# Turning cached keys on VectorE instead of TensorE, and an earlier split of the samples' sums, in a hybrid streaming layer

## The chip, the cores and the metric

The kernel runs on one core of one Trainium2 chip. A core has five engines that work in parallel, each through its own instructions in order: TensorE (PE in the profile; its weight loads are PEld), VectorE (DVE), ScalarE (ACT), GpSimd (POOL) and SyncE (SP), which here issues nearly all DMA transfers. The metric is the device time of one execution in microseconds (us), the median of several runs.

## The reference

One step of one encoder layer for two streams at once: 512 prompt frames without a cache, and 64 sample frames with 512 cached frames. Cut to the parts around the change:

```python
def stick_breaking(q, k, v, q_pos, k_pos):
    z = einsum('bqhd,bkhd->bhqk', q, k) / sqrt(HEAD_DIM)          # float32
    mask = k_pos[None, :] < q_pos[:, None]
    log_1mb = where(mask, log_sigmoid(-z), 0.0)
    after = cumsum(log_1mb, axis=3, reverse=True) - log_1mb
    w = where(mask, exp(log_sigmoid(z) + after), 0.0)
    return einsum('bhqk,bkhd->bqhd', w, v)

hn = rmsnorm(x, g_norm1)
q, k, v, gb, gc, hc = split(hn @ w_in)          # 8 heads x 128; 1024 convolution channels
q, k = rmsnorm(q, g_q), rmsnorm(k, g_k)
o_attn = stick_breaking(q, concat(k_past, k), concat(v_past, v), ...)
o_conv = gb * causal_conv3(gc * hc)
x = x + concat(rmsnorm(o_attn), rmsnorm(o_conv)) @ w_out
x = x + (silu(h2 @ w_gate) * (h2 @ w_up)) @ w_down                # h2 = rmsnorm(x)
```

The model width is 2048 and the feed-forward width 5632. Everything is float32. The cached keys come as `cache_k` with 512 frames x 8 heads x 128 and are already normed.

## The kernel before

Frames lie along the free axis (576 = 512 + 64 columns, two halves of 288), channels along the 128 partitions. A float32 matrix is split into a high part of reduced precision (a cast on ACT) and a remainder (a subtraction on DVE), and a product is three matmuls of parts; the helper `split` (lines 226 to 229) does cast and subtraction. Time passes in three stages: the input projection, then attention together with the output projection, then the feed-forward network.

PE's instructions stand in the order in which the program writes them. Those of the other engines are ordered by a scheduler when the kernel is built. PE's order is made by a small queue of generators, `Pipeline`: each group of three projection matmuls (line 223) is one tick, and a generator that yields n is resumed n ticks later.

In the attention stage the convolution half of the output projection supplies the ticks: products `pjo` of `mixc` with the weights `whi` and `wlo`. One generator `attend(h)` runs per head, a new one every 29 ticks. For the prompt it makes scores in blocks of 128 keys, block 2 together with 3 first (tile `z2`), then 1 (`z1`) and 0 (`z0`), takes a softplus of each on ACT (three activations, lines 1116 to 1118) and DVE (line 1119), masks and sums on POOL, and splits the results (`ph`, `pl`). Then it makes the samples' scores `zs` (line 1189) against the new keys and the cached keys `kcT`, and their softplus and running sums in `sp` (tile `hbl`; POOL lines 1193 to 1197). Later the sums along the keys are made by matmuls with triangular matrices (lines 1223 to 1243 for the prompt, 1204 to 1207 for the samples, from the split sums `sph` and `spl`), `weights(b)` masks on DVE (line 1214), takes the Exp on ACT (line 1216) and splits again, and the values are weighed (`po`, line 1268, and line 1282).

`split_qk` splits the queries and keys of the next head into `qh`, `ql`, `kh`, `kl`. `load_cached_keys(h)` brings a head's cached keys with one DMA as four blocks of 128 frames x 128 channels into `cK`. `keys_cached(h)` (line 1140) turns these blocks to channels x frames by four transposes on PE into a PSUM tile, copies that to `kcT` on ACT (line 1143) and asks for the keys of the next head. For the first head it is called after the scores of block 1, for each later one from the head before it, between the samples' softplus and the sums. The samples' sums are split behind the weights of block 1.

SP has eight semaphores for its transfers in turn, so a transfer waits for the landing of the eighth before it, and whatever stands behind a waiting request on SP waits too.

Of the kernel before, what the change touches and what calls it, by code (L numbers as in the profile page):

```python
# [10 lines left out]
F32 = mybir.dt.float32  # L11
# [5 lines left out]
P = 128  # L17
TP = 512
TS = 64
T = TP + TS  # L20
HALF = T // 2
HALVES = ((0, HALF), (HALF, T))
D = 2048
KD = D // P
NH = 8
# [10 lines left out]
NFP = NFF // 2  # L36
DC = D // 256
SLOTS = 7
# [63 lines left out]
def tile_hybrid_stream_step(  # L102
# [6 lines left out]
    nc = tc.nc  # L109
# [3 lines left out]
    ck, cv = cache_k[0, 0], cache_v[0, 0]  # L113
# [23 lines left out]
    ps_pj = ctx.enter_context(tc.tile_pool(name="ps_pj", bufs=3, space=PSUM))  # L137
    ps_z = tc.alloc_tile_pool(name="ps_z", bufs=1, space=PSUM)

    def misc(name):  # L140
        return ps_z.tile([P, 512], F32, tag="misc", name=name, bufs=2)
# [3 lines left out]
    for half in (1, 0):  # L145
        for c in range(D // 256):
            specs.append((w_out[half * AW : (half + 1) * AW, c * 256 : (c + 1) * 256]
# [46 lines left out]
    def next_weight():  # L194
        i = pos[0]
        pos[0] += 1
        end = first_block
        def pieces_of(j):
            hi, lo = weight_split(j)
            for a in range(0, 2048, 512):  # L200
                weight_parts(raws[j][:, :2048], hi, lo, a, a + 512, nc.vector)
                yield 7

        while len(raws) < min(i + 2, end):
            load_weight()
        if len(ready) <= i:
            split_weight(nc.vector)
        while len(raws) < min(i + 3, end):
            load_weight()
        if i + 1 < end:  # L210
            pipe.spawn(pieces_of(i + 1))
            pipe.run_due()
        out = ready[i]
        ready[i] = None
        return out
# [10 lines left out]
    def split(hi, lo, src, lo_eng=None):  # L226
        cast = nc.scalar.copy(out=hi, in_=src)  # L227
        (lo_eng or nc.vector).tensor_tensor(out=lo, in0=src, in1=hi.bitcast(F32), op=ALU.subtract)  # L228
        return cast.ins
# [6 lines left out]
    ident = const.tile([P, P], F32, name="ident")  # L236
# [312 lines left out]
    def turn_x(kt, low=None):  # L549
# [25 lines left out]
        if q == 0:  # L575
            for (a, b), d in zip(HALVES, (b11[:, j], b12a[:, j] if j < NP - 1 else b12b)):
                nc.scalar.activation(out=d[:, 0, :], in_=st[:, 0, a:b], func=AF.Copy, scale=g)
# [54 lines left out]
    with tc.manual_schedule(engines={mybir.EngineType.Activation, mybir.EngineType.DVE, mybir.EngineType.SP}):  # L632
# [60 lines left out]
        for kt in range(KD + LAG):  # L693
# [22 lines left out]
            if kt in (7, 11, 17):  # L716
                j = (kt - 7) // 4
# [7 lines left out]
        for c in range(2):  # L725
            for i, (a, b) in enumerate(HALVES):
                if i:
# [12 lines left out]
        for kt in range(KD):  # L740
# [6 lines left out]
            if kt == 9:  # L747
                nc.vector.reduce_sum(out=ssr, in_=ssx, axis=mybir.AxisListType.X)
                nc.vector.tensor_scalar(out=ssr, in0=ssr, scalar1=1.0 / D, scalar2=EPS, op0=ALU.mult, op1=ALU.add)
                nc.gpsimd.tensor_tensor(out=rst, in0=ssr, in1=nhalf, op=ALU.pow)  # L750
# [15 lines left out]
    for c in range(2):  # L766
        for i, (a, b) in enumerate(HALVES):
            nc.scalar.copy(out=e1[c][:, a:b], in_=v1ps[c][i])
# [81 lines left out]
    def group_scale(acc_, bufs):  # L850
        for a, b in HALVES:
            ss = misc("ssg")[:, :HALF]
            mm(ss, oner.bitcast(F32), acc_[:, a:b], start=True, stop=True)
            yt = tmp.tile([P, 2, HALF], F32, tag="hl", name="ytg", bufs=bufs)
            y, t = yt[:, 0], yt[:, 1]
            nc.scalar.activation(out=ss, in_=ss, func=AF.Identity, scale=1.0 / (8 * P), bias=epsc)
            nc.scalar.activation(out=y, in_=ss, func=AF.Ln)
            nc.scalar.activation(out=y, in_=y, func=AF.Exp, scale=-0.5)
            nc.scalar.activation(out=t, in_=y, func=AF.Square)
            nc.vector.scalar_tensor_tensor(out=t, in0=t, scalar=-0.5, in1=ss, op0=ALU.mult, op1=ALU.mult)  # L860
            nc.vector.scalar_tensor_tensor(out=acc_[:, a:b], in0=t, scalar=1.5, in1=y, op0=ALU.add, op1=ALU.mult)
            yield 1
# [11 lines left out]
    def a_done(n, c, i, ps, part):  # L874
        kind, g = UNITS[n][:2]
        a, b = HALVES[i]
        if kind in ("v", "qk"):
# [125 lines left out]
    bpool = tc.alloc_tile_pool(name="bpool", bufs=1, reuse_waits="tile", side="left")  # L1003
    qf, kf = (bpool.tile([P, T], F32, name=name) for name in ("qf", "kf"))
    qh, ql, kh, kl = (bpool.tile([P, TP], F32R, name=name) for name in ("qh", "ql", "kh", "kl"))
    cK = bpool.tile([P, 4, P], F32, name="cK")
    ws = bpool.tile([P, 320], F32, name="ws")
    kcT = bpool.tile([P, TP], F32, name="kcT")
    neg1r, trir = (bpool.tile([P, P], F32R, name=name) for name in ("neg1r", "trir"))
# [4 lines left out]
    sph, spl = (bpool.tile([P, T], F32R, name=name) for name in ("sph", "spl"))  # L1014
# [9 lines left out]
    def split_qk():  # L1024
        split(qh, ql, qf[:, :TP])
        split(kh, kl, kf[:, :TP])

    def load_cached_keys(h):
        nc.sync.dma_start(out=cK, in_=ck[:, h, :].rearrange("(i p) d -> p i d", p=P))

    def fetch_v(h):
        nc.sync.dma_start(out=vtok, in_=v_dram[h])
# [2 lines left out]
    load_qk(0)  # L1035
    split_qk()
    load_cached_keys(0)
    fetch_v(0)
    nc.vector.tensor_scalar(out=neg1r, in0=ident, scalar1=0.0, scalar2=-1.0, op0=ALU.mult, op1=ALU.add)
# [27 lines left out]
    for h in range(NH):  # L1067
        t = tpool.tile([P, 2, T], F32R, tag=f"t{h}", name=f"mixa{h}")
# [5 lines left out]
    def out_proj(frame, R, after=None, before=None, first=None):  # L1074
        for c in range(D // 256):
            whi, wlo = first[0] if first and c == 0 else next_weight()
            load_x2()
            if before:
                before(c)
            for j in range(2):  # L1080
                kt = 2 * c + j
                for a, b in HALVES:
                    if first and kt == a == 0:
                        ps = first[1]
                    else:
                        ps = ps_pj.tile([P, HALF], F32, tag="pj", name="pjo")
                        product(ps, whi, wlo, slice(j * P, (j + 1) * P), frame, 8, a, b)
                    if first and c < PLAIN:
                        nc.vector.tensor_tensor(out=x2(kt)[:, a:b], in0=ps, in1=R[:, a:b], op=ALU.mult)
                        continue  # L1090


                    def finish_out(wait, ps=ps, kt=kt, a=a, b=b):
                        yield wait
                        nc.vector.tensor_tensor(out=ps, in0=ps, in1=R[:, a:b], op=ALU.mult)
                        nc.vector.tensor_tensor(out=x2(kt)[:, a:b], in0=ps, in1=x2(kt)[:, a:b], op=ALU.add)

                    pipe.spawn(finish_out(3 if after and kt == a == 0 else 0))
                    pipe.run_due()
                if first and j and c < PLAIN:  # L1100
                    nc.gpsimd.dma_start(out=x2t[c], in_=xt_dram[2 * c : 2 * c + 2].rearrange("k p t -> p k t"),
                                        accum_op=ALU.add)
                if after:
                    after(kt)
# [32 lines left out]
        split(bt["vh"][2], bt["vl"][2], vtok[:, 2, :])  # L1137

    def keys_cached(h):
        kc = ps_pj.tile([P, 512], F32, tag="pj", name="kc")  # L1140
        for i in range(4):
            nc.tensor.transpose(kc[:, i * P : (i + 1) * P], cK[:, i, :], ident)
        nc.scalar.copy(out=kcT, in_=kc)
        if h + 1 < NH:
            load_cached_keys(h + 1)

# [3 lines left out]
    def attend(h):  # L1150
        pr, ph, pl, s1h, s1l, sp = (bt[n] for n in ("pr", "ph", "pl", "s1h", "s1l", "sp"))
# [60 lines left out]
        def weights(b):  # L1212
            for i in ((2, 3) if b == 2 else (b,)):
                nc.vector.scalar_tensor_tensor(out=zb[i][:, :P], in0=zb[i][:, :P], scalar=0.0, in1=mneg,
                                               op0=ALU.min, op1=ALU.add)
            nc.scalar.activation(out=pr[b][:, : full[b]], in_=z[b][:, : full[b]], func=AF.Exp)
            return split(ph[b], pl[b], pr[b][:, : width[b]])

        yield 1
        if h + 1 < NH:  # L1220
            keys_cached(h + 1)
        yield 2
        mm(zb[3], trif, pb[3], stop=False, **kw)
        mm(zb[2][:, P:], neg1f, pb[3], stop=False, **kw)
        mm(zb[2], trir, ph[2], stop=False, **kw)
# [1 line left out]
        behind = weights(2)  # L1227
        if h + 1 < NH:
            with tc.issue_after(behind):
                split_qk()  # L1230
        yield 4
        mm(zb[1], trir, ph[1], stop=False, **kw)
        mm(zb[1], trir, pl[1], stop=False, **kw)
        mm(zb[1][:, P:], neg1r, s1h, stop=False, **kw)
        mm(zb[1][:, P:], neg1r, s1l, stop=True, **kw)
        behind = weights(1)
        with tc.issue_after(behind):
            split(sph, spl, sp)
        yield 4
        mm(zb[0], trir, ph[0], stop=False, **kw)  # L1240
        mm(zb[0], trir, pl[0], stop=False, **kw)
# [50 lines left out]
    def heads():  # L1292
        yield 9
        open_b()
        yield 3
        for h in range(NH):
            pipe.spawn(attend(h))
            yield PERIOD
# [86 lines left out]
    def before_b2(c):  # L1385
        if c == 3:
            load_columns([("B", 0), ("B", 1)])
        elif c == D // 256 - 2:
            load_columns([("A", 0)])
# [305 lines left out]
```

## Time and profile before

| | us |
|---|---|
| median of 3 runs | 2347.15 |
| lowest and highest | 2346.91, 2348.15 |
| the profiled execution, its own time | 2347.48 |
| its span | 2345.8 |
| PE busy in the span | 2332.0 (99%) |
| DVE busy | 1940.0 (83%) |
| ACT busy | 1239.2 (53%) |
| POOL busy | 294.2 (13%) |

The span runs from the first to the last instruction of the profiled execution. Busy times of engines overlap. The granted clock of TensorE was 1.0 as a mean of the execution. The heads' matmuls lie between about 585 and 760 us.

A row of a timeline has the start from the beginning of the span, the length, the engine, the source line, the operation, the tile written and those read, the shapes, and in brackets the idle time of the engine before it and what ended it. Matmuls are pipelined: one lasts longer than the distance to the next one's start.

### The profile page before, as it was taken

Reading aid. Unit: us, or ns where it says so; the run is one execution under the profiler, and the core shown is the slowest. Engines: PE = TensorE matmul, PEld = TensorE weight load, DVE = VectorE, ACT = ScalarE, POOL = GpSimd, SP = SyncE. Lnnn points to the kernel's source line nnn. Section 1 sums busy time; section 2 is a strip of 40 time slices with the busy share of each in tenths; the row PEclk is TensorE's granted clock in tenths of the full one; section 3 lists DMA queues with packets and bytes.
Section 4 is the critical chain, followed back from the end, with each engine's and each line's share of the span. In section 5 each row is a group of like instructions: output and inputs, shape, how many; then the busy total and the mean of one; then the engine's idle time right before and its main releaser. Section 6 shows DMA issues by size and latency. Waiting matters only on the chain. (4 is left out here: it accounts for less than half of the span.)

```text
span 2345.8 us, 43802 instructions
## 1 busy us (share of the span) xinstructions
PE 2332.0 (99%) x17561; PEld 2321.6 (99%) x17561; DVE 1940.0 (83%) x2834; ACT 1239.2 (53%) x2244; POOL 294.2 (13%) x374
## 2 busy tenths in 40 slices
PE   9999999999999999999999999999999999999999
PEld 8999999999999999999999999999999999999998
DVE  8889889797777898888888888888888778887875
ACT  8556656455887564444444444444444444444454
POOL 0211121120332320000000000000000002431211
PEclk9999999999999999999999999999999999999999
DMA  8444243436753454444444444444444937875642
GB/s 270 137 122 123 90 142 103 149 116 208 202 143 109 168 198 126 154 141 136 154 128 149 148 134 149 138 139 153 127 150 140 356 112 229 231 218 187 201 130 82
DMA packets 482867, 368.85 MB, mean 157 GB/s; under 512 B 11630, under 2 KB 465064, under 8 KB 482664
## 3 DMA queue, kind: packets, MB, share of 16 engines
q1 hardware_dynamic: 475848, 356.58, 47.5%
q0 software_dynamic: 6384, 9.21, 2.3%
q8 instruction: 137, 2.24, 0.4%
q14 instruction: 66, 0.54, 0.1%
q10 hardware_dynamic: 432, 0.27, 0.0%
HBM read 285.52 MB, written 80.49 MB: 156 GB/s over the span
## 5 line engine op out<-in xcount | busy, mean ns | idle before, releaser
L228 DVE TENSOR_TENSOR whl<-raw_a,whl 128x1024 fp32r<-128x1024 f32 (+4 forms) x384 | 435.8, 1135 | 61.2 <-ACT whl L227 59.9
L404 PE MATMUL psy<-t,whl 128*128 128x288 f32 x3000 | 449.8, 295 | 0.0
L227 ACT CAST whl<-raw_a 128x1024 fp32r<-128x1024 f32 (+4 forms) x384 | 360.0, 939 | 137.7 <-PE psx L404 46.4
L404 PE MATMUL psy<-h_s,whl 128*128 128x288 f32 x2766 | 417.4, 295 | 0.6 <-ACT part L427 0.6
L404 PEld LDWEIGHTS psy<-t,whl 128*128 128x128 f32 x3000 | 414.8, 188 | 0.2
L404 PE MATMUL psw<-t,whl 128*128 128x288 f32 x2688 | 390.3, 295 | 0.0
L404 PEld LDWEIGHTS psy<-h_s,whl 128*128 128x128 f32 x2766 | 383.7, 188 | 1.2 <-ACT part L427 1.1
L404 PEld LDWEIGHTS psw<-t,whl 128*128 128x128 f32 x2688 | 367.0, 188 | 0.2
L228 DVE TENSOR_TENSOR whl<-raw_b,whl 128x1024 fp32r<-128x1024 f32 (+5 forms) x234 | 253.3, 1083 | 88.0 <-ACT whl L227 87.1
L227 ACT CAST whl<-raw_b 128x1024 fp32r<-128x1024 f32 (+5 forms) x234 | 211.0, 904 | 211.0 <-issue 75.2
L427 ACT COPY part<-psy 128x288 f32<-128x288 f32 x309 | 122.8, 397 | 345.0 <-PE psy L404 343.8
L404 PE MATMUL psx<-h_s,whl 128*128 128x288 f32 x1164 | 170.9, 295 | 0.0
L227 ACT CAST whl<-s 128x1024 fp32r<-128x1024 f32 (+5 forms) x103 | 95.2, 925 | 122.8 <-PE psw L404 115.0
L404 PEld LDWEIGHTS psx<-h_s,whl 128*128 128x128 f32 x1164 | 159.8, 188 | 0.0
L404 PE MATMUL psy<-t12a,whl 128*128 128x288 f32 x1056 | 150.9, 296 | 0.0
L404 PE MATMUL psw<-t34a,whl 128*128 128x288 f32 x1056 | 150.6, 295 | 0.0
L404 PEld LDWEIGHTS psy<-t12a,whl 128*128 128x128 f32 x1056 | 143.5, 188 | 0.3
L404 PEld LDWEIGHTS psw<-t34a,whl 128*128 128x128 f32 x1056 | 143.7, 188 | 0.0
L228 DVE TENSOR_TENSOR whl<-s,whl 128x1024 fp32r<-128x1024 f32 (+5 forms) x103 | 109.8, 1066 | 20.2 <-ACT whl L227 19.5
L1439 POOL DMA_DIRECT2D hid_dram<-form x7 | 5.2, 738 | 954.1 <-DVE form L228 945.8
L223 PE MATMUL pjo<-mixc,whi 128*128 128x288 f32 x512 | 119.0, 300 | 0.0
L223 PE MATMUL pjo<-mixa,whi 128*128 128x288 f32 x512 | 102.8, 296 | 0.0
(591 smaller groups left out, 3953.3 us busy)
## 6 DMA issues: line engine op xcount, KB each, us to landing
hid_dram<-form SPq DMA_DIRECT2D x147, 288.0 KB, 2.8
raw_a<-in_w_in_dram SPq DMA_DIRECT2D x22, 1024.0 KB, 5.5
raw_b<-in_w_in_dram SPq DMA_DIRECT2D x22, 1024.0 KB, 6.1
raw_b<-in_w_gate_dram SPq DMA_DIRECT2D x22, 1024.0 KB, 7.8
raw_b<-in_w_up_dram SPq DMA_DIRECT2D x22, 1024.0 KB, 6.5
raw_a<-in_w_gate_dram SPq DMA_DIRECT2D x22, 1024.0 KB, 5.8
raw_a<-in_w_up_dram SPq DMA_DIRECT2D x22, 1024.0 KB, 5.5
h_s<-hid_dram SPq DMA_DIRECT2D x10, 2016.0 KB, 11.0
```

The lines of the kernel that those rows point to most:

```text
L223: mm(ps, w_[:, k, csl], x_[:, a:b], start=(k == 0 and n == 0), stop=(k == nk - 1 and n == 2))
L227: cast = nc.scalar.copy(out=hi, in_=src)
L228: (lo_eng or nc.vector).tensor_tensor(out=lo, in0=src, in1=hi.bitcast(F32), op=ALU.subtract)
L404: mm(ps, whl[:, w_, j, :], x_, start=(start and j == 0 and q == 0), stop=(j == len(xs_) - 1 and q == 2), skip_group_check=True)
L427: nc.scalar.copy(out=t, in_=st["y"])
L1439: q.dma_start(out=hid_dram[fp][2 * n - 2 : 2 * n].rearrange("f p t -> p f t"), in_=t.bitcast(F32))
```

## The change

Three things change.

1. The cached keys of a head are loaded by four DMAs instead of one. DMA number g/32 brings channels g to g+31 of all 512 frames, in pieces of 32 numbers (128 bytes), so that `cK` holds 4 x 16 blocks of 32 frames x 32 channels, each where its turned form belongs.
2. One DVE instruction, `nc.vector.transpose`, turns all blocks of 32 x 32 in place and writes `kcT`. The four transposes on PE, the PSUM tile `kc` and the copy on ACT are gone.
3. In `attend`, `keys_cached(h + 1)` is called after the weights of block 2 and after the split of the samples' sums, and that split stands behind the Exp and cast of block 2 instead of block 1. The two yields of 1 and 2 ticks become one of 3; ticks do not move.

```diff
+BK = 32
-    cK = bpool.tile([P, 4, P], F32, name="cK")
+    cK = bpool.tile([P, TP], F32, name="cK")
     def load_cached_keys(h):
-        nc.sync.dma_start(out=cK, in_=ck[:, h, :].rearrange("(i p) d -> p i d", p=P))
+        for g in range(0, P, BK):
+            nc.sync.dma_start(out=cK[g : g + BK].rearrange("j (t d) -> j t d", d=BK),
+                              in_=ck[:, h, g : g + BK].rearrange("(t j) d -> j t d", j=BK))
     def keys_cached(h):
-        kc = ps_pj.tile([P, 512], F32, tag="pj", name="kc")
-        for i in range(4):
-            nc.tensor.transpose(kc[:, i * P : (i + 1) * P], cK[:, i, :], ident)
-        nc.scalar.copy(out=kcT, in_=kc)
+        nc.vector.transpose(out=kcT, in_=cK)
         if h + 1 < NH:
             load_cached_keys(h + 1)
...
-        yield 1
-        if h + 1 < NH:
-            keys_cached(h + 1)
-        yield 2
+        yield 3
         mm(zb[3], trif, pb[3], stop=False, **kw)
...
         if h + 1 < NH:
             with tc.issue_after(behind):
                 split_qk()
+        with tc.issue_after(behind):
+            split(sph, spl, sp)
+        if h + 1 < NH:
+            keys_cached(h + 1)
         yield 4
         mm(zb[1], trir, ph[1], stop=False, **kw)
...
-        behind = weights(1)
-        with tc.issue_after(behind):
-            split(sph, spl, sp)
+        weights(1)
         yield 4
```

`tc.issue_after(behind)` keeps what is recorded inside it behind the instruction `behind`, here the cast of the block's Exp.

## The prediction

> **What bounds the kernel now.** I read the page first, then the busy time of the attention stretch, then TensorE's (PE's) waits there, then the timelines of single engines.
>
> ```profile
> span 2345.8 us, 43802 instructions
> PE 2332.0 (99%) x17561; PEld 2321.6 (99%) x17561; DVE 1940.0 (83%) x2834; ACT 1239.2 (53%) x2244; POOL 294.2 (13%) x374
> ```
>
> PE is busy for all but 13.8 us of the span. The profiled execution took 2347.48 us, 1.7 us more than its span and 0.33 us more than the median of the runs (2347.15 us). I make the sum against the profiled execution and carry its difference over to the median. The edit touches only the 180 us in which the eight heads run between the output projection's matmuls:
>
> ```profile
> 580.00:760.00 180.00, 178.13 (x1301) 172.57 (x1300) 133.69 (x280) 141.22 (x319) 57.22 (x106) 1.00 0.53 157
> ```
>
> The columns are the stretch, its length and the busy time of PE, weight loads, DVE, ACT and POOL, then granted clock, DMA share, GB/s. PE leaves 1.9 us idle; DVE is busy 74% of the time, ACT 78%. So time can be won here only by giving PE fewer instructions or by ending its waits. The waits (total, times, longest):
>
> ```profile
> PE zs L1205 <- DVE spl L228: 1.0, 3, 0.4
> PE z L1161 <- DVE kl L228: 0.3, 1, 0.3
> PE zs L1204 <- ACT sph L227: 0.3, 1, 0.3
> ```
>
> **Part 1, the 32 transposes on PE go.** One head's set in PE's timeline (start, length):
>
> ```profile
> 617.65 0.30 PE L223 MATMUL pjo<-mixc,whi 128*128 128x288 f32 x1
> 617.78 0.60 PE L1142 MATMUL kc<-ident,cK 128*128 128x128 f32 x4
> 618.13 0.38 PE L223 MATMUL pjo<-mixc,whi 128*128 128x288 f32 x1
> 618.35 0.30 PE L223 MATMUL pjo<-mixc,wlo 128*128 128x288 f32 x1
> ```
>
> Projection matmuls follow each other by 0.13 us (617.65 to 617.78). With the set between them, the next but one starts 0.57 us after 617.78; without it, 0.13 us after. A set costs 0.44 us, eight cost 3.5 us. PE's written order is otherwise untouched. The copy out of PSUM goes from ACT too:
>
> ```profile
> L1143 ACT COPY kcT<-kc x8: 561/576/583, 591.9 to 724.2; 128x512 f32<-128x512 f32 x8
> ```
>
> That frees 0.58 us of ACT a head, which is not the bound, and I count it at nothing.
>
> **Part 2, the samples' split moves ahead of the second block.** `spl` is what PE waits for at L1205 and `sph` at L1204. In heads 1 to 6 the changed build has `sph` directly behind `kh` on ACT and `spl` directly behind `kl` on DVE, so both leave their queues before the Exp, cast and subtraction of block 1, about 1 us earlier. The waits were at most 0.4 us each: 1.3 us gone. What is late next there is `kl`:
>
> ```profile
> 625.21 0.68 DVE L228 TENSOR_TENSOR kl<-kf,kh 128x512 fp32r<-128x512 f32 x1
> 626.17 0.28 PE L1161 MATMUL z<-qh,kl 128*128 128x256 f32 x1
> ```
>
> It ends at 625.89, 0.28 us before PE uses it, and nothing new stands ahead of it in those heads. The gain side is therefore 3.5 + 1.3 = 4.8 us, 0.20% of the time, and it cannot be much more, since all of PE's idle time in the stretch is 1.9 us.
>
> **Part 3, the transposes on DVE.** No DVE transpose is in this trace. The nearest rows are DVE instructions on as many float32 elements, such as the 0.68 us above. I take 0.69 us. Below I allow 0.5 us, since a copy reads one operand and not two; above, 2.4 us, in case the turn takes four such passes, which no row excludes. From the third on, the transpose also waits until PE has read the old `kcT`, with `s0l` and block 0's maximum queued behind it on DVE; the built order puts it just ahead of `s0l`.
>
> ```profile
> 613.23 1.06 PE L1189 MATMUL zs<-qf,kcT 128*128 128x64 f32 x8
> 616.36 0.56 DVE L228 TENSOR_TENSOR s0l<-hbl,s0h 128x384 fp32r<-128x384 f32 x1 [1.39 <-ACT s0h L227]
> ```
>
> PE is done reading at 614.3, and DVE sits idle for 1.39 us until 616.36: that gap covers 0.69 us, and the wait with it. Without that cover the transpose would push `s0l` and what follows by its own length. In head 0 there are two on the path.
>
> The first: scores of the samples need `kcT`, and DVE reaches the transpose behind the split of block 2.
>
> ```profile
> 591.75 0.42 DVE L228 TENSOR_TENSOR hbe<-pr,hbe 128x256 fp32r<-128x256 f32 x1 [1.11 <-ACT hbe L227]
> 592.85 1.06 PE L1189 MATMUL zs<-qf,kcT 128*128 128x64 f32 x8
> ```
>
> It runs from 592.17 to 592.86. PE, 0.44 us earlier than before, wants the result at 592.41: a wait of 0.45 us, which eats the first set's gain.
>
> The second is behind the split of block 1, and here the order of head 0 matters. Casts of q and k for head 1, which stood ahead of the Exps of blocks 1 and 0, are now placed by the scheduler behind them. In the changed build, ACT's order from the samples' cast on is
>
> ```
> sph, Exp z1, ph1, qh, Exp z0, kh
> ```
>
> and DVE's is
>
> ```
> spl, pl1, transpose, z0 mask, evacuation, wlo, ql, kl
> ```
>
> PE's scores of head 1 need `kh` and `kl`, so they now hang on a chain that begins with POOL's sums for the samples, which stood behind them before:
>
> ```profile
> 601.56 1.70 POOL L1197 TENSOR_TENSOR hbl<-hbl 128x64 f32<-128x64 f32 x3
> 603.05 0.62 ACT L227 CAST kh<-kf 128x512 fp32r<-128x512 f32 x1
> 603.57 0.48 ACT L1216 ACTIVATE hbl<-z 128x384 f32<-128x384 f32 x1
> 604.08 0.51 ACT L227 CAST ph<-hbl 128x384 fp32r<-128x384 f32 x1
> 604.50 0.67 ACT L227 CAST sph<-hbl 128x576 fp32r<-128x576 f32 x1
> 604.40 0.68 DVE L176 TENSOR_TENSOR wlo<-raw_a,whi 128x512 fp32r<-128x512 f32 x1
> 605.00 0.55 DVE L228 TENSOR_TENSOR pl<-hbl,ph 128x384 fp32r<-128x384 f32 x1
> 606.14 0.28 DVE L1214 SCALAR_TENSOR_TENSOR z<-z,mneg 128x128 f32<-128x128 f32 x1
> 606.34 0.44 DVE L1089 TENSOR_TENSOR x<-pjo,accc 128x288 f32<-128x288 f32 x1
> 605.66 0.28 PE L1161 MATMUL z<-qh,kh 128*128 128x256 f32 x1
> 605.78 0.27 PE L1161 MATMUL z<-qh,kl 128*128 128x256 f32 x1
> ```
>
> POOL is done at 603.3. From there, by the distances between starts in these rows: `sph` to 603.9, Exp z1 to 604.4, `ph1` to 604.9 on ACT; `pl1` from 605.0 to 605.5 and the transpose to 606.1 on DVE; the z0 mask to 606.3, evacuation to 606.7, `wlo` to 607.3, `ql` to 607.9, `kl` to 608.6. (On ACT, Exp z0 and `kh` end at 607.6, so PE's first score would start then and stop again for `kl`.) PE wants `kl` at 605.78 less 0.44, at 605.34. The stall is 608.6 less 605.34, 3.3 us. Were all of ACT and DVE a little earlier in head 0 it would be 2; if POOL's sums slip, which hang on a softplus that now stands behind a weight cast, 4.5. I take 3.3.
>
> **Part 4, the loads.** One request of 512 pieces of 512 bytes becomes four requests with 2048 pieces of 128 bytes in all.
>
> ```profile
> cK<-in_cache_k_dram SPq DMA_DIRECT2D x8, 256.0 KB, 2.9
> raw_a<-in_w_in_dram SPq DMA_DIRECT2D x22, 1024.0 KB, 5.5
> SPq L1029 <- PE kc L1142: 15.8, 6, 3.2
> 581.77 0.43 SPq L1029 DMA_DIRECT2D cK<-in_cache_k_dram  x1
> ```
>
> The weight load in the second row is 2048 pieces of 512 bytes (128 columns of float32). So four times as many pieces land in 2.9 to 5.5 us, and three more issues of SP at 0.43 us come on top: 4.2 to 6.8 us. A head's keys are asked for when the head before has been turned, some 20 us earlier, so I count it at nothing; in head 0 the second load has the 12 us from 592.9 to 605.5. On SP, the requests behind the keys' (q, k and weights of the next head) now wait for DVE instead of PE, at nearly the same moments. The Trainium skill, "DMA: Bandwidth & Descriptors", section "Specifications", speaks against the smaller pieces: full rate wants at least 512 bytes. By that rule a load would be dearer; with the cover of 12 us the sum would stay as it is even at twice 5.5 us.
>
> **Sum.** -3.5 - 1.3 + 0.45 + 3.3 = -1.05 us. From the median of 2347.15 us that makes **2346.1 us**, 0.04% faster. About 0.2% (4.7 us) is what a measurement of this kernel can tell from no change.
>
> **Rivals.**
>
> *The gain arrives whole.* If head 0's chain is shorter than I think, since POOL ends sooner or `kl` gets through, nothing is paid: 2347.15 - 4.8 = 2342.3 us. For it: PE's idle time falls in every other head. Against it: the order in head 0 is fixed at build, and its links have measured lengths. Chance 0.08.
>
> *The transpose is dear, and the kernel gets slower.* Place: DVE. In head 0 each microsecond over 0.69 counts twice, once ahead of the samples' scores and once ahead of `kl`. At 2.4 us that is 3.4 us more. In six further heads it no longer fits the 1.39 us gap, and what stands behind it comes 1.0 us late, `kl` among it with 0.28 us of slack; if half of the 0.7 us beyond is made up on the way, each head pays 0.4 us, 2.4 us more. Together 2346.1 + 5.8 = 2351.9 us, slower by 0.2%. It decides from a transpose of about 2.2 us on; up to 1.2 us the time stays within a microsecond of no change. For it: no row shows the instruction. Against it: DVE rows of this size all take 0.7 us. Chance 0.14.
>
> *PE's clock falls in the stall.* Only one stretch of this trace shows a granted clock under 1, the one at the end in which PE is idle half the time:
>
> ```profile
> 2335.00:2346.00 11.00, 5.59 (x43) 5.00 (x41) 0.92 (x2) 2.28 (x9) 2.82 (x5) 0.93 0.26 74
> ```
>
> If the 3.3 us stall lowered the clock to half for as long again, PE would lose 1.7 us: 2347.8 us. Against it: the stall is broken by a matmul. The Trainium skill, "TensorE: Matmul & The Clock Gate", section "What's actually happening", has such a rule: after an idle window of about 3.4 us the clock is halved. No run so far shows it inside a head. Chance 0.06.
>
> *The change doesn't do what it says* as far as the split is concerned: in head 0 `sph` waits for POOL and delays block 1 instead of using a gap. That is part of my forecast and has no chance of its own.
>
> **How the numbers follow.** My forecast (stall of 2 to 4.5 us) has 0.72 and gives 2344.8 to 2347.4; with a transpose between 0.5 and 1.2 us, 2344.4 to 2348.3. Faster by over 0.2% needs the whole gain and a little more: 0.07. Slower by over 0.2% needs the dear transpose or a stall over 9 us: 0.14. Within 0.2%: 0.79. The range for 8 in 10 leaves out the far ends of both rivals: 2342.8 to 2350.5.
>
> **What would show it.** Right: a DVE transpose of about 0.7 us; no PE wait on `spl` at the samples' sums in heads 1 to 7; one wait of PE of 2 to 4.5 us at the first scores of head 1, put down to `kh` or `kl`, and about 0.45 us at the first samples' scores; later heads 0.44 us shorter each. Wrong: waits of PE on DVE in every head, a transpose over 1.2 us, SP or DVE waiting for the keys' load, or no wait at all in head 0.

## The result, and the profile after

The changed kernel takes 2349.38 us (median of 21 runs, 2347.60 to 2352.61), the kernel before in the same series 2346.53 us (21 runs, 2345.24 to 2348.62). The ratio is 1.0014, with a 95% interval of 1.0008 to 1.0020: slower by 2.85 us, 0.12%, by the medians. That lies inside the forecast range and within 0.2% of no change, but on the other side of it: a gain of 1 us was forecast, and a loss of 3 us came. The profiled execution of the changed kernel took 2350.66 us, 3.18 us more than that of the kernel before.

The page of the changed kernel, its first lines:

```profile
span 2349.0 us, 43773 instructions
PE 2331.3 (99%) x17529; PEld 2320.5 (99%) x17529; DVE 1943.7 (83%) x2842; ACT 1235.1 (53%) x2236; POOL 295.0 (13%) x374
```

PE has 32 instructions fewer and less busy time, as it should, and yet the span is 3.2 us longer: PE's idle time grew from 13.8 to 17.7 us. The stretches of the changed kernel (start and end, length, then busy time of PE, weight loads, DVE, ACT and POOL, granted clock, DMA share, GB/s):

```profile
580.00:760.00 180.00, 174.85 (x1255) 168.80 (x1254) 134.75 (x284) 136.14 (x309) 56.16 (x106) 0.99 0.56 155
600.00:620.00 20.00, 17.06 (x110) 16.16 (x109) 13.41 (x29) 13.91 (x32) 5.65 (x13) 0.91 0.64 161
608.00:610.00 2.00, 1.52 (x9) 1.52 (x10) 1.02 (x2) 0.73 (x2) 0.00 (x0) 0.79 0.78 123
610.00:612.00 2.00, 2.00 (x10) 2.00 (x9) 0.44 (x2) 0.98 (x3) 0.00 (x0) 0.50 0.99 321
612.00:614.00 2.00, 2.00 (x13) 2.00 (x12) 0.68 (x2) 1.13 (x3) 1.05 (x3) 0.85 0.48 161
```

In the heads' 180 us PE is idle for 5.2 us, where it was 1.9. In the 20 us around the start of head 1 it is idle for 2.9 us, and the granted clock there is 0.91. The three short rows place it: 0.5 over the whole of 610 to 612 us, and partly in the stretches on both sides. What is missing to full speed is 0.21, 0.50 and 0.15 of 2 us, 1.7 us of work, or some 3.4 us at half the clock.

PE's waits in the heads' stretch (total, times, longest):

```profile
PE z L1161 <- ACT kh L228: 2.3, 1, 2.3
PE po L1267 <- ACT ph L228: 1.3, 3, 0.7
PE z L1161 <- DVE kl L229: 1.0, 2, 0.6
PE zs L1189 <- DVE kcT L1143: 0.3, 1, 0.3
```

The waits on `spl` and `sph` are gone. In their place are one on `kh` and `kl` at the first scores of head 1 (2.3 and 0.6 us), three on `ph` where block 1's or block 0's weights meet the values, one more of 0.4 us on `kl` in a later head, and one on the turned keys at the first samples' scores. The 0.3 us on `kl` that the kernel before shows lie at 587.7 us in its head 0, ahead of everything that the edit changes.

The same place in PE's timeline (start, length, instruction, and in brackets the idle time before it), then in ACT's and in DVE's:

```profile
604.86 0.29 PE L224 MATMUL pjo<-mixc,whi 128*128 128x288 f32 x1
607.47 0.38 PE L1161 MATMUL z<-qh,kh 128*128 128x256 f32 x1 [2.31 <-ACT kh L228]
608.48 0.39 PE L1161 MATMUL z<-qh,kl 128*128 128x256 f32 x1 [0.63 <-DVE kl L229]
```

ACT's:

```profile
603.26 0.67 ACT L228 CAST sph<-hbl 128x576 fp32r<-128x576 f32 x1 [0.84 <-POOL hbl L1197]
603.84 0.48 ACT L1216 ACTIVATE hbl<-z 128x384 f32<-128x384 f32 x1
604.36 0.51 ACT L228 CAST ph<-hbl 128x384 fp32r<-128x384 f32 x1
604.77 0.61 ACT L228 CAST qh<-qf 128x512 fp32r<-128x512 f32 x1
606.31 0.60 ACT L1216 ACTIVATE pr<-z 128x512 f32<-128x512 f32 x1 [0.92 <-DVE z L1214]
606.80 0.61 ACT L228 CAST kh<-kf 128x512 fp32r<-128x512 f32 x1
```

DVE's:

```profile
604.90 0.56 DVE L229 TENSOR_TENSOR pl<-hbl,ph 128x384 fp32r<-128x384 f32 x1 [0.18 <-ACT ph L228]
605.38 0.71 DVE L1143 STREAM_TRANSPOSE kcT<-cK 128x512 f32<-128x512 f32 x1
606.00 0.27 DVE L1214 SCALAR_TENSOR_TENSOR z<-z,mneg 128x128 f32<-128x128 f32 x1
...
607.14 0.68 DVE L229 TENSOR_TENSOR ql<-qf,qh 128x512 fp32r<-128x512 f32 x1
607.74 0.69 DVE L229 TENSOR_TENSOR kl<-kf,kh 128x512 fp32r<-128x512 f32 x1
```

The chain on which the forecast built its stall is here link by link: the samples' cast waits for POOL's sums, `kh` is last of six on ACT, and `kl` last of seven on DVE (the rows left out are the evacuation and `wlo`). `kl` ends at 608.4 us; 608.6 was worked out.

The turn itself, by the view of the tile it writes (shortest, median and longest ns, first and last start):

```profile
L1143 DVE STREAM_TRANSPOSE kcT<-cK x8: 700/706/712, 591.7 to 721.6; 128x512 f32<-128x512 f32 x8
```

The keys' requests on the page (count, KB each, median us to landing):

```profile
cK<-in_cache_k_dram SPq DMA_DIRECT2D x32, 64.0 KB, 4.2
```

SP's timeline where head 1's keys and then its queries are asked for:

```profile
592.44 2.93 SPq L1031 DMA_DIRECT2D cK<-in_cache_k_dram  x4
595.47 0.43 SPq L1022 DMA_DIRECT2D qf<-qk_dram  x1
```

The turn takes 0.71 us every time. Queries of head 1, asked for behind the keys, are on their way from 595.5 us on. Such a request lands 4.5 us after its issue (median), the one for `kf` behind it 4.9 us, and the casts start only at 604.8 us, `qh` without idle time of ACT before it, `kh` behind an Exp that waits for DVE's mask. So it is not the data that is late there but the place in ACT's queue.

How far each matmul of PE has moved shows where the time went. The table takes the same matmul, counted in PE's order without the transposes, and gives its start less its start in the kernel before, in us, from the traces of PE. The last column is the second experiment.

```
start before, matmul                            after    late request
 587.69  scores of head 0, ahead of any turn    -0.39    -1.00
 592.55  behind the first set of transposes     -0.80    -1.50
 592.96  samples' scores, behind the wait       -0.33    -1.03
 605.53  last projection ahead of head 1        -0.67    -1.38
 605.66  head 1, z<-qh,kh                       +1.81    -1.38
 605.78  head 1, z<-qh,kl                       +2.70    -1.38
 608.07  projection, some 2.3 us on             +4.21    -1.32
 617.25  projection, clock back at 1.00         +4.40    -1.32
 660.15  projection, after three more heads     +2.05    -3.47
 670.62  po<-pl                                 +2.90    -2.97
 753.39  po<-ph, last head                      +2.36    -3.52
 886.52  feed-forward                           +1.91    -4.22
1997.73  feed-forward                           +3.03    -3.42
```

From -0.39 to +2.36 the heads' stretch costs 2.75 us. The rest of the 3.2 us lies in stages that the edit does not touch, where single executions differ: 0.45 us less at 886.5 us and 1.1 us more at 1997.7 us, both at waits on a copy out of PSUM. The 2.75 us are made of eight sets of transposes at 0.44 us that are gone (-3.5), 0.45 us at the first turned keys (-0.80 to -0.33, of which 0.3 us is idle time), 3.4 us at head 1's first scores (-0.67 to +2.70), 1.7 us while the clock is halved (+2.70 to +4.40), and what is left, 0.7 us more for waits in the later heads.

### The profile page after: what moved, and what is told of

It reads as the page before. It is cut to its first block, busy times and chain, and to the rows that moved or that the text cites. A ratio compares the mean times of both kernels' runs of the same rounds, so it can differ in the third digit from the quotient of the medians.

```text
span 2349.0 us, 43773 instructions
## 1 busy us (share of the span) xinstructions
PE 2331.3 (99%) x17529; PEld 2320.5 (99%) x17529; DVE 1943.7 (83%) x2842; ACT 1235.1 (53%) x2236; POOL 295.0 (13%) x374
```

## The experiments

The theory: in head 0 the scheduler placed the casts of q and k behind the Exps of blocks 1 and 0 because the small pieces of the keys' request, which stands ahead of q's and k's on SP, count as slow in its plan; the stall at head 1's first scores is made by that order, and the clock falls as its consequence. Rivals: the earlier split makes the stall; DVE's turn costs the time in every head; the loads are late on the chip. All ratios below are against runs of the kernel before on the same chip, 5 rounds each, with 95% intervals; 0.001 is 2.3 us.

### The changed kernel again

> The changed kernel once more, beside the next three. Theory A (the loss sits between head 0 and head 1: the scheduler, faced with four key loads, puts the casts of q and k for head 1 behind the Exp of block 0, PE stalls for about 2.9 us and then runs 3.4 us at half clock): 1.001 to 1.002 of before. Rival B (the loss sits in all heads, because the samples' split ahead of block 1 delays ph0 and PE waits for it): the same ratio, but waits of PE on ph would add up to 3 us or more.

2349.41 us (11 runs) against 2346.50: 1.0011, 1.0002 to 1.0020. The same four waits (2.3, 1.2, 1.0 and 0.3 us) and a clock of 0.91 from 600 to 620 us. So neither the loss nor the stall is chance.

### The keys of head 1 asked for later

```diff
     def keys_cached(h):
         nc.vector.transpose(out=kcT, in_=cK)
-        if h + 1 < NH:
+        if 0 < h < NH - 1:
             load_cached_keys(h + 1)
...
         if h + 1 < NH:
             load_qk(h + 1)
+        if h == 0:
+            load_cached_keys(1)
```

The request for head 1's keys stands behind that for head 1's q and k, and not ahead of it. Nothing else is edited.

> The changed kernel with one edit: the cached keys of head 1 are asked for behind the queries and keys of head 1 instead of ahead of them, which puts the casts qh, kh of head 1 back ahead of the Exps of blocks 1 and 0 in the built order. Theory A: no wait of PE on kh or kl at the first scores of head 1, granted clock 1.00 there, 4 to 5 us less than the changed kernel, 0.9985 to 0.9995 of before. Rival B: about as slow as the changed kernel, 1.0005 to 1.0015. Rival C (small pieces of 128 bytes hold up the loads behind them): as the changed kernel.

2344.32 us: 0.9993, 0.9984 to 1.0002. Its waits of PE in the heads' stretch:

```profile
PE po L1269 <- ACT ph L228: 1.2, 3, 0.7
PE z L1161 <- DVE kl L229: 0.4, 1, 0.4
PE zs L1189 <- DVE kcT L1143: 0.3, 1, 0.3
```

Its timelines in head 0, ACT and then PE's first score of head 1:

```profile
602.16 0.62 ACT L228 CAST kh<-kf 128x512 fp32r<-128x512 f32 x1
602.68 0.67 ACT L228 CAST sph<-hbl 128x576 fp32r<-128x576 f32 x1
...
604.28 0.28 PE L1161 MATMUL z<-qh,kh 128*128 128x256 f32 x1
```

Moving one request puts `qh` and `kh` back ahead of `sph`; the wait on `kh` is gone, and with it the fall of the clock (1.00 in the heads' stretch). Against the changed kernel that is 5.1 us: the stall's 3.4 and the clock's 1.7. The waits on `ph` stay, so they have another cause. Rival C is not tested by this edit, since head 1's q and k no longer stand behind the keys' requests here; what speaks against it is the changed kernel's ACT, which reaches `qh` without waiting for its data.

A second series of the same kernel, since the interval reached past 1:

> The kernel of the late request for head 1's keys a second time, for the interval of its ratio to the kernel before. If its gain is the -2.2 us first measured (the eight sets of transposes, -3.5 us, less the waits on ph and kl that come instead of those on spl), the median lies at 2344.0 to 2345.2 us again, 0.9989 to 0.9995 of the kernel before, with no wait on kh at head 1's first scores. If the first ratio was luck, it lies within 0.5 us of the kernel before (0.9998 to 1.0002).

2344.52 us (11 runs) against 2346.76: 0.9991, 0.9982 to 1.0000. Both series give -2.2 us. This version is faster than the changed kernel; that it is faster than the kernel before is likely but not settled, since both intervals reach 1.

### One request with large pieces

```diff
     def load_cached_keys(h):
-        for g in range(0, P, BK):
-            nc.sync.dma_start(out=cK[g : g + BK].rearrange("j (t d) -> j t d", d=BK),
-                              in_=ck[:, h, g : g + BK].rearrange("(t j) d -> j t d", j=BK))
+        nc.sync.dma_start(out=cK.rearrange("p (i d) -> p i d", d=P),
+                          in_=ck[:, h, :].rearrange("(i p) d -> p i d", p=P))
```

The keys come as in the kernel before, in one request with pieces of 512 bytes, and DVE turns them as they lie; blocks of cached keys then stand in other places than the samples' scores need.

> The changed kernel with the keys loaded by one request in pieces of 512 bytes as before; the blocks then lie in other places than the turn wants, so scores against cached keys are not those of the reference, while every instruction's size stays. In its built order qh, kh of head 1 stand ahead of the Exps. Theory A: no wait on kh, clock 1.00, 0.9985 to 0.9995, as the variant with the later keys. If the turn or the split were the cause: 1.001 as the changed kernel.

2343.05 us: 0.9985, 0.9976 to 0.9994. The built order of head 0 has `qh` and `kh` early again, with the request in its old place; PE does not wait on `kh`, nor on the first turned keys:

```profile
PE po L1265 <- ACT ph L228: 1.2, 3, 0.7
PE z L1159 <- DVE kl L229: 0.4, 1, 0.4
```

So two different edits of the request, a later place and larger pieces, both restore the order and take the stall away. That the scheduler's plan holds the small pieces for slow is a reading that fits both, but it is not shown: the plan's own figures are not in the record, and the number of requests changed together with the size of the pieces, so four requests instead of one would fit as well. This kernel also shows what the turn on DVE and the earlier split bring with the load of before: 3.5 us (interval 1.4 to 5.6).

### The earlier split alone, and the turn alone

The kernel before with only the new place of the split (its four transposes and the copy stay, called where they were):

```diff
         if h + 1 < NH:
             with tc.issue_after(behind):
                 split_qk()
+        with tc.issue_after(behind):
+            split(sph, spl, sp)
         yield 4
...
-        behind = weights(1)
-        with tc.issue_after(behind):
-            split(sph, spl, sp)
+        weights(1)
```

> The kernel before with the early split of the samples' sums alone, keys turned by TensorE as before. The prediction's part 2: 1.3 us less, 0.9994. Theory A with B's mechanism at a small size (waits of PE move from spl to ph0 and kl): 0 to 1.5 us more, 1.0000 to 1.0006. In either case no wait of PE over 1 us between head 0 and head 1, and clock 1.00.

2346.36 us: 0.9999, 0.9990 to 1.0008. Its waits of PE in the heads' stretch:

```profile
PE po L1268 <- ACT ph L227: 0.7, 1, 0.7
PE po L1268 <- DVE pl L228: 0.2, 1, 0.2
```

No wait on `kh`: the earlier split does not make the stall. The waits on `spl` and `sph` (1.3 us before) have gone, and 0.9 us on block weights have come. The medians differ by 0.1 us; by PE's starts the heads gain 0.5 us (-1.07 at 587.69 and -1.60 at 753.39, read like the table above).

The changed kernel with call and split in their old places, so that loads and turn alone are new:

```diff
-        yield 3
+        yield 1
+        if h + 1 < NH:
+            keys_cached(h + 1)
+        yield 2
...
-        with tc.issue_after(behind):
-            split(sph, spl, sp)
-        if h + 1 < NH:
-            keys_cached(h + 1)
         yield 4
...
-        weights(1)
+        behind = weights(1)
+        with tc.issue_after(behind):
+            split(sph, spl, sp)
```

> The kernel before with the four loads and the turn by VectorE alone; call and samples' split at their old places, no mending of the order. In its built order the casts qh, kh of head 1 still stand behind the Exps (kh behind that of block 0), but the samples' cast stands behind block 1's. Theory A: a wait of PE at the first scores of head 1 of 1.5 to 2.5 us, so the early split makes only part of it; 0.9990 to 1.0000 without and up to 1.0007 with a half-clock stretch. Rival D (the early split alone makes the stall in head 0): no such wait, 0.9985 to 0.999 as in the mended variant with the old split.

2348.93 us: 1.0010, 1.0001 to 1.0019, more than the 1.0007 that was expected at most. Its longest wait of PE:

```profile
PE z L1161 <- ACT kh L228: 2.4, 1, 2.4
```

Its stretch around the start of head 1:

```profile
600.00:620.00 20.00, 17.28 (x113) 16.52 (x112) 13.14 (x27) 14.11 (x33) 5.96 (x14) 0.91 0.69 175
```

The stall and the fall of the clock are there without the earlier split, in nearly full size, and the earlier split alone has neither. Since turn and split with one request of large pieces have neither as well, they belong to the four requests of small pieces.

The same with the later request for head 1's keys, that is, the second experiment's kernel with call and split in the old places:

> As the one before, and the samples' split and the call for the keys at their old places: of the change only the four loads and the turn by VectorE are left. Theory A: 3.1 us less than before (eight sets of 0.44 us less one wait of 0.4 us), 0.9985 to 0.999; the waits on spl of the kernel before (1.3 us) stay. If rival B holds beside A, this one is 1 to 2 us faster than the variant with the early split; if the early split gains what the prediction gave it, 1.3 us slower.

2344.92 us: 0.9992, 0.9984 to 1.0001. Its waits on the samples' sums:

```profile
PE zs L1207 <- DVE spl L229: 1.3, 3, 0.6
PE zs L1206 <- ACT sph L228: 0.7, 2, 0.4
```

They were 1.3 us in the kernel before and are 2.0 us here. The gain of 3.1 us that was expected did not come whole: the medians give 1.6 us, PE's starts over the heads 2.15 us (-0.46 to -2.61). Half of the 2.0 us lies in head 3. DVE there, around the turn:

```profile
654.06 0.70 DVE L1143 STREAM_TRANSPOSE kcT<-cK 128x512 f32<-128x512 f32 x1
656.51 0.56 DVE L229 TENSOR_TENSOR s0l<-hbl,s0h 128x384 fp32r<-128x384 f32 x1 [1.75 <-ACT s0h L228]
```

The turn is done 1.75 us before DVE's next step can start, so it is hidden in this head. What differs is that PE comes to these sums 3.0 us earlier than in the kernel before, and ACT's cast `sph` only 1.75 us earlier (666.25 instead of 668.00): PE has run ahead by the transposes and waits that are gone, and meets the engines that feed it. The other heads were not traced for this. The earlier split exchanges these 2.0 us for 1.2 us on `ph`, and the two medians (2344.92 and 2344.32) differ by less than the intervals.

### Samples' remainder on POOL

To see whether DVE's queue is what holds the waits of the later heads, `spl` is subtracted on POOL in the kernel with the later request:

```diff
         with tc.issue_after(behind):
-            split(sph, spl, sp)
+            split(sph, spl, sp, nc.gpsimd)
```

> The variant with the later keys, with the samples' remainder spl subtracted by POOL instead of VectorE. If the waits of PE on ph0 and kl in the later heads come from spl standing ahead of block 0's mask on VectorE: these waits (1.2 and 0.4 us) go, 1 to 1.5 us less than that variant, 0.9982 to 0.999. If they come from ScalarE's cast sph: they stay, no difference. Against it: POOL takes about 1.5 us for it, and its masks for the next head wait behind.

2344.76 us: 0.9992, 0.9983 to 1.0001. Its waits:

```profile
PE z L1161 <- DVE kl L229: 1.8, 3, 1.0
PE z L1161 <- ACT kh L228: 0.5, 1, 0.5
PE po L1269 <- ACT ph L228: 0.3, 1, 0.3
```

The waits on `ph` fall from 1.2 to 0.3 us and those on `kl` and `kh` rise from 0.4 to 2.3 us; no gain. Neither expectation came true, so this does not settle which queue holds the later heads.

### Three ticks of projection ahead of head 1

```diff
             pipe.spawn(attend(h))
-            yield PERIOD
+            yield PERIOD + 3 * (h == 0)
```

Nine projection matmuls more stand between heads 0 and 1, in the changed kernel, so that PE has work where it stalled.

> The changed kernel with three more ticks (nine projection matmuls, 1.2 us of PE work) between the start of head 0 and that of head 1; the built order of head 0 stays. It shortens PE's idle time before the first scores of head 1 without taking away the late casts. If the idle time itself halves the clock (a rule with a threshold near 3 us): idle 1.7 to 2 us left, clock 1.00 there, 2.5 to 3 us less than the changed kernel, 1.0000 to 1.0003. If the half clock has another cause: 1.2 us less or nothing (the last head then ends three ticks later), clock under 1 there, 1.0005 to 1.0012.

2349.76 us: 1.0013, 1.0004 to 1.0022, slower than either expectation had it. Its stretches around the start of head 1 and at the end of the last head:

```profile
600.00:620.00 20.00, 19.29 (x140) 18.52 (x140) 14.81 (x32) 15.69 (x37) 7.33 (x15) 1.00 0.59 153
752.00:760.00 8.00, 7.11 (x31) 6.17 (x31) 6.24 (x12) 3.67 (x10) 0.00 (x0) 0.57 0.80 197
```

Its waits of PE that grew or are new (0.6 and 1.1 us of the first row, and the second row, lie between 749 and 755 us):

```profile
PE po L1267 <- ACT ph L228: 2.0, 3, 1.1
PE zs L1281 <- ACT ws L1210: 0.9, 1, 0.9
```

At head 1 it did what was meant: PE idles 0.7 us instead of 2.9, the clock stays at 1.00, and from 690 to 752 us each matmul, counted in PE's order, starts 3.2 to 3.9 us ahead of the kernel before. But the nine matmuls are missing at the end, where PE then waits on `ph` and `ws`, and there the clock falls, to 0.57 as a mean of 8 us: 3.4 us of work lost. Filled in one place, the gap opened in another, and the clock fell there too. For the cause it speaks twice: with the stall the clock's fall left head 1, and where PE idled instead, the clock fell.

## Why the prediction was wrong

**The stall (Part 3), right.** Forecast 3.3 us, with `kl` done at 608.6; measured 3.4 us of delay, with `kl` done at 608.4. That the built order of head 0 costs that much is shown by the later request and by the large pieces.

**The clock, the rival that came true.** It had a chance of 0.06 and a price of 1.7 us; the clock fell in the changed kernel's profile, in its second series and in the turn alone, and took 1.7 us by PE's starts and by the clock rows. The price was right. The step that failed is the weight: "the stall is broken by a matmul" was taken as a reason against it. The two pieces of idle time, 2.31 and 0.63 us with one matmul between, were enough. The Trainium skill, "TensorE: Matmul & The Clock Gate", section "What's actually happening", gives the window over which activity is watched as 3413 ns and has the clock halved after at least one idle window. The trace agrees with the length, for the clock is halved for 3.4 us (609.2 to 612.6), and it shows that the window need not be idle throughout: of the 3.4 us before that PE was idle for 2.3 us. With this rival in the sum the forecast would have been 2347.8 us, still 1.6 us under the median; the rest is the later heads.

**The earlier split (Part 2), wrong by most of its size.** Forecast -1.3 us; alone it gives -0.1 us by the medians (interval -2.3 to +1.9, which cannot tell the two apart) and -0.5 us by PE's starts. The waits on `spl` did go, as forecast; 0.9 us on `ph` and `pl` came in their place. The failed step is the list of what is late next. It named `kl` alone, with "nothing new stands ahead of it", and left out block 1's weights, which the same edit pushes behind; and it took PE's own place as fixed, though PE comes earlier by every wait that is gone. ACT and PE of the changed kernel at the sums of head 3, then ACT of the kernel before:

```profile
669.26 0.67 ACT L228 CAST sph<-hbl 128x576 fp32r<-128x576 f32 x1
669.83 1.66 ACT L176 CAST whi<-raw_a 128x512 fp32r<-128x512 f32 x3
...
671.78 0.58 ACT L1216 ACTIVATE pr<-z 128x512 f32<-128x512 f32 x1
672.25 0.51 ACT L228 CAST ph<-hbl 128x384 fp32r<-128x384 f32 x1
...
672.81 0.62 PE L1267 MATMUL po<-ph,hbe 128*128 128x384 f32 x2 [0.35 <-ACT ph L228]
```

```profile
667.58 0.51 ACT L227 CAST ph<-hbl 128x384 fp32r<-128x384 f32 x1
668.00 0.67 ACT L227 CAST sph<-hbl 128x576 fp32r<-128x576 f32 x1
```

The samples' cast is early now; three weight casts and both Exps follow, and block 1's cast `ph` ends only when PE already waits for it. In the kernel before, the same `ph` stood ahead of `sph` and of block 0's Exp, and ended at 668.1 us, 2.2 us before PE used it at 670.3. Of that slack and the wait of 0.35 us, 2.5 us together, the two instructions now ahead of it take 0.9 us (from the start of the cast `kh` to the end of `ph` it is 4.0 us instead of 3.1). The rest is PE, which has come closer to ACT: `kh` is cast 3.8 us later than in the kernel before, and PE's scores come only some 2 us later. `kl` did become late too, by 0.4 us in one later head.

**The turn (Part 3) in the later heads.** Its length is right, 0.71 us against 0.69. That the gap on DVE covers it is so in the head that was looked at. But the forecast counted the turn's part in the later heads at nothing, and with the split in its old place it is about +0.9 us by PE's starts (-2.15 us measured, where the sets and the first turned keys give -3.5 + 0.45): PE, without its transposes, waits 2.0 us on the samples' sums instead of 1.3. How much of this the turn makes and how much PE's running ahead was not separated.

**Transposes and first scores, right.** A set is worth 0.44 us where nothing else moves (+4.40 to +3.96 at the third set), and the first turned keys delay PE by 0.45 us, both as forecast.

**The loads (Part 4).** From the first of head 1's four requests (592.4 us) to the landing of the last (597.5 us) it is 5.1 us, inside the estimate of 4.2 to 6.8; the 4.2 us on the page are those of a single request. The four issues took 2.93 us on SP, 0.73 us each where 0.43 was assumed, which cost nothing here: no engine waits for the data. What they cost is in the built order, not on the chip. That the order in head 0 changes was read from the build; that it changes because of the loads was not looked for.

**The sum.** For the heads' stretch, by the forecast: -3.5, -1.3, +0.45 and +3.3, -1.05 us. By the trace: -3.5, +0.45, +3.4 and +1.7 for the clock, and what is left to the measured +2.75 is +0.7 for all waits of the later heads, where -1.3 stood. The clock (1.7 us) and the later heads (2.0 us) are nearly the whole error of 3.8 us. The dear transpose, the rival for a slower kernel, is out: the loss came from a stall that the forecast had right, from a clock that it set aside, and from a gain that did not come.

## What to carry to other kernels

Where a scheduler orders the engines when the kernel is built, an edit can act through the plan alone: compare the built orders around every request that changes its pieces, and where a step falls back in a queue, try the request in another place before giving the edit up. Price a stall of TensorE of 2 to 3 us with the clock that may follow it, here half as much again, even if a single matmul breaks it. When work is moved ahead in a queue, list everything that now stands behind it, not only the next step that was tight. And when the bounding engine is given less to do, count the slack of what feeds it from its new, earlier place.

## What was not expected of the hardware

The granted clock fell to 0.5 for 3.4 us after 2.9 us of idle time in two pieces, and began to fall only when PE was already working again: PE resumed at 608.5 us, the half-microsecond from 609.0 to 609.5 us has 0.67, and the row of 610 to 612 us has 0.50. The idle time need not fill the 3.4 us before the fall: PE was idle for 2.3 us of them in the changed kernel, for 1.9 us in its second series, and for 1.7 us in the kernel with nine matmuls more, where two waits of 0.6 and 1.1 us at the end of the last head were followed by half the clock for 6.8 us, a mean of 0.57 over the 8 us shown; a third wait of 0.9 us fell into that time. A single wait of 1.3 us in the feed-forward stage of the kernel before (at 886.5 us) and one of 1.0 us at head 1 in the kernel with the remainder on POOL left the clock at 1.00. How much idle time it takes, and whether its place in time matters, was not tried on its own.
